# Attention values of a two-layer encoder: the values' projection turned round, with transposes to token order

## The chip, the cores and the metric

The kernel runs on one core of a Trainium2 chip. What is measured is the time of one execution on the device, in microseconds (us); lower is better. The core has a matrix engine (PE), whose loading of stationary operands is shown as an engine of its own (PEld), a vector engine (DVE), a scalar engine (ACT), GpSimd (POOL), and DMA queues that are fed by the sync engine (SP) and by ACT. A matmul holds one operand of at most 128 columns in the array (the stationary one, "weights" of the array) and streams the other through it (the moving one); it writes to PSUM, in banks of 512 float32 per partition. In the profile a matmul is written `out<-moving,stationary`.

## The reference, cut to what matters

Two requests of 512 tokens and 1,024 features go through a two-layer encoder. Layer 0 projects the normed input h with one matrix `w_in` (queries, keys, values, and a Hyena part), lets three groups of four heads attend in dilated windows, and merges the groups:

```python
proj = h @ p['w_in']
qkv = proj[..., :3 * ATTN_WIDTH].reshape(B, L, 3, N_PATTERNS, ATTN_HEADS_PER_GROUP, HEAD_DIM)
for g, (window, dilation) in enumerate(ATTN_PATTERNS):        # (128, 1), (512, 4), (2048, 16)
    o, lse = _dilated_window_attention(qkv[:, :, 0, g], qkv[:, :, 1, g], qkv[:, :, 2, g],
                                       slopes[g], window, dilation)
```

The values of one group are a 1,024 x 256 projection: `ATTN_WIDTH` is 768, `HEAD_DIM` is 64. Layer 1 is an RWKV-7 scan in both directions; each layer ends in a convolutional feed-forward part (FFN). Everything is float32.

## The kernel before

All activations lie feature-major: a tile is 128 features x 512 tokens, and eight tiles make one request's 1,024 features. A projection is `dense` (lines 119 to 130): it loads a block of weights, 128 output features wide, and for each of the eight feature chunks k runs three matmuls, because each float32 operand is split into a high and a low part (`mm3`: high x high, low x high, high x low). Weights are stationary, 512 tokens stream: 24 matmuls per 128 outputs, in one PSUM bank of the pool `psd` (tag `pd`, three banks, shared by both requests). `load_w` (line 97) brings a block of 512 KB by a DMA on ACT's queue into one of two `wraw` buffers; ACT rounds it to the high part `whi`, POOL subtracts to get the low part `wlo`.

Attention (`attention`, line 440) goes through six parts: group g = 0, 1, 2 by head pair hp = 0, 1. `project(g, hp)` makes queries and keys of a part (two calls of `dense`) and, where hp is 0, the values V of the whole group. V is wanted token-major (128 tokens x 256 features, four blocks b), since it is the stationary operand of the product with the attention weights. So the values' projection (lines 453 to 469) swaps the roles: h is stationary, 128 tokens of it at a time, and 256 columns of the weights (`wva`) stream. For g = 0 the 128 tokens of a block lie side by side; for g = 1 and 2 a block takes every fourth token (`perm`, line 343), so the stationary operand is read with a step of four. The four blocks fill two PSUM banks `pv` of the pool `psd`, which are held from the first matmul to the last of the 96, and are then copied to V by ACT (line 469).

`attend` (line 485) makes scores of a head in PSUM (`ps<-qk,qk`), DVE adds the distance penalty into a tile `sb` (three buffers) and takes the row maximum, ACT takes the exponential in place, PE transposes `sb` block by block, the transposed block `pt` is copied out, and PE multiplies it with V (`ps<-pt,V`).

Two requests, s = 0 and 1, run as generators that yield the estimated PE time of what they issued. `weave` and `run` interleave them by these estimates: while part n attends, part n + 1 is projected; beside the attention of request 0 runs the conditioning (`ada_params`, matmuls `ps<-adaw,sc`, fed by 512 KB transfers on SP's queue), and beside that of request 1 the output projection and FFN of request 0. The list of tiles so issued is then ordered once more, engine by engine, by a scheduler that knows each operation's inputs and buffers; within an engine, work is done strictly in that order.

Of the kernel before, what the change touches and what calls it, by code (L numbers as in the profile page):

```python
# [8 lines left out]
F32 = mybir.dt.float32  # L9
# [8 lines left out]
L = 512  # L18
NS = 2
T = NS * L  # L20
KC = D // 128
# [16 lines left out]
def _vec_layout():  # L38
    at = 0
    for name, n in (("adab0", 48), ("adab1", 48), ("n1_0", 8), ("n2_0", 8), ("n1_1", 8), ("n2_1", 8), ("fin", 8),  # L40
# [3 lines left out]
        VEC[name] = at  # L44
        at += n
    return at
# [5 lines left out]
class K:  # L52
# [387 lines left out]
    def attention(self, s, hs, ap, op, then, early):  # L440

        nc, a = self.nc, self.a
        xs = lambda k: hs[k]
        nd = op.tile([128, 3, 4, 2, 4], F32, name="nd")
        z = op.tile([128, 516], F32, name="places")
        nc.sync.dma_start(z, a["places"])
        nm, den = nd[:, :, :, 0], nd[:, :, :, 1]
        rel = ap.tile([128, 640], F32, name="rel")
        nc.sync.dma_start(rel, a["rel"])
        O, V, qk = {}, {}, {}  # L450

        def project(g, hp):
            if hp == 0:
                V[g] = ap.tile([128, 4, 256], F32, tag="V", bufs=2, name="V")
                pv = [self.psd.tile([128, 512], F32, tag="pd", name="pv") for _ in range(2)]
                for i in range(2):
                    wh, wl = self.load_w(a["wva"][g, :, i * 4:i * 4 + 4], 4, 256)
                    for k0 in (0, 2):
                        for b in range(4):
                            o = pv[b // 2][:, b % 2 * 256:b % 2 * 256 + 256]  # L460
                            for k in (k0, k0 + 1):
                                first, last = i + k + b % 2 == 0, i + k == 4
                                hh, hl = (self.perm(t, g, b) for t in hs[i * 4 + k])
                                self.mm(o, hh, wh[k], start=first, stop=False, skip_group_check=True)
                                self.mm(o, hl, wh[k], start=False, stop=False, skip_group_check=True)
                                self.mm(o, hh, wl[k], start=False, stop=last, skip_group_check=True)
                    yield 48 * 109
                for b in range(0, 4, 2):
                    nc.scalar.copy(V[g][:, b:b + 2], pv[b // 2].rearrange("p (b c) -> p b c", b=2))
            qk[g, hp] = []  # L470
            for i, m in enumerate((g * 2 + hp, 6 + g * 2 + hp)):
                t = ap.tile([128, L], F32, tag=f"qk{i}", bufs=2, name=f"qk{i}")
                qk[g, hp].append(t)
                yield from self.dense(a["win"][m], KC, xs, lambda ps: nc.scalar.activation(t, ps, AF.Copy, scale=0.125 if i == 0 else 1.0))

        parts = [(g, hp) for g in range(3) for hp in range(2)]
        yield from project(*parts[0])
        for (g, hp), nxt in zip(parts, parts[1:]):
            yield from self.weave(project(*nxt), self.attend(ap, g, hp, qk[g, hp], V[g], rel, nm, den, O, op))
        early()  # L480
        g, hp = parts[-1]
        yield from self.weave(then, self.attend(ap, g, hp, qk[g, hp], V[g], rel, nm, den, O, op))
        self.at_out = nd, z, O
# [847 lines left out]
def _blocks(np, w, m):  # L1331

    k, n = w.shape
    return np.ascontiguousarray(w.reshape(k // 128, 128, n // m, m).transpose(2, 1, 0, 3))


def layout(np, i):
    _vec_layout()
    o = {}
    x = np.concatenate([i["x_prompt"][0], i["x_sample"][0]], 0)  # L1340
    o["xT"] = np.ascontiguousarray(x.T.reshape(KC, 128, T).transpose(1, 0, 2))
    c = np.concatenate([i["c_prompt"], i["c_sample"]], 0)
    o["cT"] = np.ascontiguousarray(c.T.reshape(KC, 128, NS).transpose(1, 0, 2))
    vec = np.zeros((128, NV), np.float32)

    def put(name, arr, rows=128):
        arr = np.asarray(arr).reshape(-1, rows)
        vec[:rows, VEC[name]:VEC[name] + arr.shape[0]] = arr.T

    for l in range(2):  # L1350
        p = f"l{l}_"
        o[f"adaw{l}"] = _blocks(np, i[p + "ada_w"], 512)
        o[f"up{l}"] = _blocks(np, i[p + "ffn_up"], 128)
        o[f"dn{l}"] = _blocks(np, i[p + "ffn_down"], 128)
        put(f"adab{l}", i[p + "ada_b"])
        put(f"n1_{l}", i[p + "norm1"])
        put(f"n2_{l}", i[p + "norm2"])
        put(f"cw{l}", i[p + "ffn_conv_w"])
        put(f"cb{l}", i[p + "ffn_conv_b"])
    put("fin", i["final_norm"])  # L1360
    put("sw", i["l0_short_w"])
    put("sb", i["l0_short_b"])
    put("fbias", i["l0_filt_bias"])
    for n, m in (("fb1", "filt_b1"), ("fb2", "filt_b2"), ("fb3", "filt_b3"), ("freq", "filt_freq")):
        put(n, i["l0_" + m], 64)
    for n, m in (("mu", "mu"), ("w0", "w0"), ("a0", "a0"), ("kk", "k_k"), ("ka", "k_a"), ("rk", "r_k"), ("lnw", "ln_w"), ("lnb", "ln_b")):
        put(n, i["l1_" + m])
    fw = np.full((8, 128), 2.0 ** -9, np.float32)
    fw[0, 0] = 2.0 ** -10
    fw[4, 0] = 2.0 ** -10  # L1370
    put("fw", fw)
    put("rest", np.where(np.arange(128) % 32 // 4 == 1, -1.0, 0.0).astype(np.float32))
    o["vecs"] = vec
    o["ident"] = np.eye(128, dtype=np.float32)
    w = i["l0_w_in"]
    o["win"] = _blocks(np, w, 128)
    o["wva"] = _blocks(np, w[:, 1536:2304], 256)
    o["wout"] = _blocks(np, i["l0_w_out"], 128)
    for n in "rkvo":
        o["w" + n] = _blocks(np, i["l1_w_" + n], 128)  # L1380
    for n in "wa":
        o[f"l{n}1"] = _blocks(np, i[f"l1_{n}1"].transpose(1, 0, 2).reshape(D, 128), 128)
    g1, g2 = i["l1_g1"], i["l1_g2"]
    o["lg1a"] = _blocks(np, g1[:, :128], 128)
    o["lg1b"] = _blocks(np, g1[:, 128:], 32)

    l2 = np.zeros((6, 128, KC, 128), np.float32)
    for j, m in enumerate((i["l1_a2"], i["l1_w2"])):
        for d in range(2):
            l2[j * 2 + d] = np.concatenate([m[d]] * 2).reshape(128, KC, 128)  # L1390
    l2[4] = g2[:128].reshape(128, KC, 128)
    l2[5, :96] = np.concatenate([g2[128:]] * 3).reshape(96, KC, 128)
    o["l2"] = np.ascontiguousarray(l2.transpose(2, 1, 0, 3))
    for n in ("filt_w1", "filt_w2", "filt_w3", "filt_w4"):
        o[n] = i["l0_" + n]
    o.update(constants(np))
    return o
# [87 lines left out]
```

## Time and profile before

| | us |
|---|---|
| median of three timed runs | 3595.82 |
| lowest and highest of them | 3590.41, 3604.41 |
| profiled execution, its own time | 3581.8 |
| its span, first to last instruction | 3580.0 |
| PE busy | 3311.5 (92%) |
| DVE, ACT, POOL busy | 1707.0, 1576.7, 1603.4 |
| mean granted clock of PE | 0.956 of full speed |

Busy time of PE is the time in which at least one matmul is under way; consecutive matmuls overlap in their ends, so how long one costs is read from the distance of two starts, not from its own duration. Attention of request 0 fills the span from 50 to about 300 us, that of request 1 from 448 to about 850 us, each with other work between.

### The profile page before, as it was taken

The page shows a single profiled execution, that of the slowest core. Times are in us where ns is not written, and L with a number is a line of the kernel's source. Part 1 is how long each engine was busy: PE and PEld are TensorE (multiplying, and loading weights), DVE is VectorE, ACT ScalarE, POOL GpSimd, SP SyncE. Part 2 cuts the span into 40 slices and gives each one's busy share as a digit, 9 for nine tenths or more (in the row PEclk, how much of TensorE's full clock was granted, in tenths as well). Part 3 has the DMA queues.
Part 4 walks back from the last instruction along what each step waited for, and adds up shares of the span by engine and source line. Part 5 has one row for each costly group of instructions (what it writes and reads, how often), then busy time and mean ns, then how long its engine had stood idle before and what let it go on. Part 6 is the DMA issues. An engine that isn't in the chain of part 4 may idle for free. (4 is left out here: it accounts for less than half of the span.)

```text
span 3580.0 us, 62660 instructions
## 1 busy us (share of the span) xinstructions
PE 3311.5 (92%) x24082; PEld 2367.3 (66%) x24082; DVE 1707.0 (48%) x3181; ACT 1576.7 (44%) x3139; POOL 1603.4 (45%) x1480
## 2 busy tenths in 40 slices
PE   7999989999999899999998897798999999989998
PEld 4555767887877676676665564466666666667776
DVE  5021442212335555386677658467677663442223
ACT  3122244434334445545556557444555454443332
POOL 2111342334435665464444557455445443444443
PEclk9999999999999999999998997798999999999999
DMA  7655141222344224654445441574444443342322
GB/s 247 227 188 192 59 136 54 76 71 86 127 132 143 97 95 165 218 155 113 115 126 135 130 121 49 198 250 152 114 113 118 127 106 94 123 159 91 97 89 88
DMA packets 378787, 463.26 MB, mean 129 GB/s; under 512 B 201239, under 2 KB 218903, under 8 KB 377080
## 3 DMA queue, kind: packets, MB, share of 16 engines
q1 hardware_dynamic: 302928, 247.78, 22.7%
q10 hardware_dynamic: 75560, 211.48, 18.6%
q8 instruction: 189, 3.10, 0.4%
q14 instruction: 110, 0.90, 0.1%
HBM read 378.11 MB, written 81.00 MB: 128 GB/s over the span
## 5 line engine op out<-in xcount | busy, mean ns | idle before, releaser
L112 POOL TENSOR_TENSOR wlo<-wraw,whi 128x512 fp32r<-128x512 f32 (+1 forms) x830 | 1086.2, 1313 | 1356.4 <-ACT whi L108 1184.7
L108 ACT CAST whi<-wraw 128x512 fp32r<-128x512 f32 (+1 forms) x830 | 497.5, 606 | 877.3 <-PE pd L78 675.8
L78 PE MATMUL pd<-midh,whi 128*128 128x512 f32 x704 | 287.9, 410 | 6.2 <-ACT midh L141 6.2
L78 PE MATMUL pd<-midl,whi 128*128 128x512 f32 x704 | 282.9, 402 | 0.9 <-DVE midl L144 0.3
L78 PE MATMUL pd<-midh,wlo 128*128 128x512 f32 x704 | 282.4, 402 | 0.3 <-POOL wlo L112 0.3
L328 DVE SCALAR_TENSOR_TENSOR x<-pd,ada,x 128x512 f32<-128x512 f32 x192 | 142.7, 746 | 196.0 <-PE pd L78 195.2
L78 PE MATMUL pd<-xml,whi 128*128 128x512 f32 (+1 forms) x448 | 191.1, 427 | 21.2 <-DVE xml L144 13.7
L78 PE MATMUL pd<-xmh,whi 128*128 128x512 f32 (+1 forms) x448 | 195.4, 438 | 5.5 <-ACT xmh L141 5.4
L78 PE MATMUL pd<-xmh,wlo 128*128 128x512 f32 (+1 forms) x448 | 186.8, 418 | 3.9 <-POOL wlo L112 3.7
L1226 POOL TENSOR_TENSOR Sg<-S,G 128x256 f32<-128x256 f32 x144 | 102.9, 714 | 169.5 <-DVE S L1224 156.2
L291 DVE SCALAR_TENSOR_TENSOR fa<-pd,vecs,fa 128x511 f32<-128x511 f32 x88 | 65.7, 746 | 231.9 <-ACT fa L290 231.9
L1211 ACT COPY UV<-X 32x128 f32<-32x128 f32 x512 | 131.6, 257 | 93.4 <-PE X L78 65.7
L321 DVE TENSOR_TENSOR fa<-fa,pd 128x512 f32<-128x512 f32 x88 | 60.4, 686 | 214.0 <-PE pd L78 202.3
L78 PEld LDWEIGHTS pd<-midh,whi 128*128 128x128 f32 x704 | 132.7, 189 | 40.6 <-ACT midh L141 9.2
L78 PEld LDWEIGHTS pd<-midl,whi 128*128 128x128 f32 x704 | 133.3, 189 | 33.4 <-DVE midl L144 4.2
L78 PEld LDWEIGHTS pd<-midh,wlo 128*128 128x128 f32 x704 | 132.9, 189 | 31.1 <-POOL wlo L112 0.7
L1224 DVE TENSOR_TENSOR S<-X,Sg 128x256 f32<-128x256 f32 x144 | 60.6, 421 | 185.1 <-ACT ys L1222 181.8
L78 PE MATMUL X<-UV,Am 32*32 32x64 f32 (+1 forms) x4096 | 127.5, 228 | 20.3 <-ACT UV L1211 17.4
L1141 DVE TENSOR_TENSOR W<-W,sub 128x120 f32<-128x120 f32 (+7 forms) x496 | 136.3, 275 | 11.1
L78 PEld LDWEIGHTS X<-UV,Am 32*32 32x32 f32 (+1 forms) x4096 | 79.0, 108 | 86.2 <-ACT UV L1211 64.3
L1139 DVE TENSOR_TENSOR sub<-U,W 128x120 f32<-128x120 f32 (+7 forms) x496 | 128.8, 260 | 14.7 <-DMA U<-inv 3.9
L78 PEld LDWEIGHTS pd<-xml,whi 128*128 128x128 f32 (+1 forms) x448 | 88.5, 198 | 53.4 <-DVE xml L144 26.2
(477 smaller groups left out, 8007.0 us busy)
## 6 DMA issues: line engine op xcount, KB each, us to landing
wraw<-in_up ACTq DMA_DIRECT2D x176, 512.0 KB, 3.5
adaw<-in_adaw SPq DMA_DIRECT2D x96, 512.0 KB, 5.2
wraw<-in_dn ACTq DMA_DIRECT2D x128, 256.0 KB, 2.7
wraw<-in_win ACTq DMA_DIRECT2D x36, 512.0 KB, 3.5
x<-x SPq DMA_DIRECT2D x48, 256.0 KB, 3.4
wraw<-in_dn ACTq DMA_DIRECT2D x64, 192.0 KB, 2.4
x<-res SPq DMA_DIRECT2D x32, 256.0 KB, 3.0
wraw<-in_wk ACTq DMA_DIRECT2D x16, 512.0 KB, 3.6
```

What stands on the lines that cost most here:

```text
L78: return self.nc.tensor.matmul(*a, **k)
L108: nc.scalar.copy(h, raw[:, o:o + w])
L112: nc.gpsimd.tensor_tensor(l, raw[:, o + p:o + p + w2], h[:, p:p + w2].bitcast(F32), ALU.subtract)
L291: nc.vector.scalar_tensor_tensor(t[:, 1:], ps[:, :L - 1], w(0), t[:, 1:], ALU.mult, ALU.add)
L321: nc.vector.tensor_tensor(act, act, ps, ALU.mult)
L328: nc.vector.scalar_tensor_tensor(x[m], ps, self.ada[l][:, 40 + m, s:s + 1], x[m], ALU.mult, ALU.add)
L1139: nc.vector.tensor_tensor(w, U4[:, :, k:, e * K + k:e * K + k + 1].to_broadcast(shape), W4[:, e:e + 1, k:k + 1, 0:k + 1].to_broadcast(shap ...
L1141: nc.vector.tensor_tensor(W4[:, :, k:, 0:k + 1], W4[:, :, k:, 0:k + 1], w, ALU.add)
L1211: nc.scalar.copy(dst, X[ur, :, uu(g)])
L1224: nc.vector.tensor_tensor(S, X[:, :, 384:512].rearrange("p d (g v) -> p d g v", g=2), self.Sg, ALU.add)
L1226: nc.gpsimd.tensor_tensor(Sg, S, self.G[:, tau, :, :, None].to_broadcast([128, 2, 2, 64]), ALU.mult)
```

## The change

The values are projected as everything else: weights stationary (blocks 12 to 17 of `win`, 128 columns each, in place of the 256-column blocks `wva`), 512 tokens streaming, 24 matmuls into one `pd` bank. ACT copies the bank to a tile `vt` in the buffers of `sb`; for g = 1 and 2 this copy brings the tokens into the order of the blocks, reading PSUM with a step of four. Four transposes on PE turn `vt` to token order in a `ps` bank, and DVE copies that into half of V. This is done twice per group.

```diff
-                pv = [self.psd.tile([128, 512], F32, tag="pd", name="pv") for _ in range(2)]
                 for i in range(2):
-                    wh, wl = self.load_w(a["wva"][g, :, i * 4:i * 4 + 4], 4, 256)
-                    for k0 in (0, 2):
-                        for b in range(4):
-                            o = pv[b // 2][:, b % 2 * 256:b % 2 * 256 + 256]
-                            for k in (k0, k0 + 1):
-                                first, last = i + k + b % 2 == 0, i + k == 4
-                                hh, hl = (self.perm(t, g, b) for t in hs[i * 4 + k])
-                                self.mm(o, hh, wh[k], start=first, stop=False, skip_group_check=True)
-                                self.mm(o, hl, wh[k], start=False, stop=False, skip_group_check=True)
-                                self.mm(o, hh, wl[k], start=False, stop=last, skip_group_check=True)
-                    yield 48 * 109
-                for b in range(0, 4, 2):
-                    nc.scalar.copy(V[g][:, b:b + 2], pv[b // 2].rearrange("p (b c) -> p b c", b=2))
+                    vt = ap.tile([128, L], F32, tag="sb", bufs=3, name="vt")
+                    yield from self.dense(a["win"][12 + g * 2 + i], KC, xs, lambda ps: nc.scalar.copy(self.unperm_src(vt, g), self.unperm(ps, g)))
+                    ps = self.ps()
+                    for b in range(4):
+                        self.tr(ps[:, b * 128:b * 128 + 128], vt[:, b * 128:b * 128 + 128], self.ident)
+                    nc.vector.tensor_copy(V[g][:, :, i * 128:i * 128 + 128], ps.rearrange("p (b c) -> p b c", b=4))
+                    yield 440
```

On PE, where the values of g = 1 of request 0 begin, the order before is this (`adam` belongs to the conditioning):

```order
L81 MATMUL ps<-ident,adam 128x128 x4
L78 MATMUL pd<-h7h,wlo 128x512
L78 MATMUL pv<-whi,h0h 128x256
L78 MATMUL pv<-whi,h0l 128x256
L78 MATMUL pv<-wlo,h0h 128x256
L78 MATMUL pv<-whi,h1h 128x256
L78 MATMUL pv<-whi,h1l 128x256
L78 MATMUL pv<-wlo,h1h 128x256
```

At the same place of the changed kernel stands:

```order
L78 MATMUL pd<-h0h,whi 128x512
L78 MATMUL pd<-h0l,whi 128x512
L81 MATMUL ps<-ident,adam 128x128 x4
L78 MATMUL pd<-h0h,wlo 128x512
L78 MATMUL pd<-h1h,whi 128x512
L78 MATMUL pd<-h1l,whi 128x512
L78 MATMUL pd<-h1h,wlo 128x512
```

The operands have changed sides, the matmuls are half as many and twice as wide; where one group of values took 96 of them, it takes 48.

A little further on PE, where group 0 of request 0 attends (`qk_...` are its keys and queries), stood before, between scores and transposes, matmuls of the values:

```order
L81 MATMUL ps<-ident,sb 128x128 x3
L78 MATMUL ps<-qk_696,qk_645 128x256
L78 MATMUL pv<-whi,h4h 128x256
L78 MATMUL pv<-whi,h4l 128x256
L78 MATMUL ps<-pt,V 64x128 x3
L78 MATMUL ps<-adaw,sc 32x512 x2
L81 MATMUL ps<-ident,sb 128x128 x2
L78 MATMUL ps<-qk_696,qk_645 128x256
```

For the second head of that part the changed kernel has:

```order
L78 MATMUL ps<-qk_669,qk_611 128x256
L78 MATMUL pd<-h7h,wlo 128x512
L81 MATMUL ps<-ident,sb 128x128 x2
L78 MATMUL ps<-qk_669,qk_611 128x384
L78 MATMUL ps<-pt,V 64x128 x2
L81 MATMUL ps<-ident,sb 128x128 x3
L78 MATMUL ps<-adaw,sc 32x512
L78 MATMUL ps<-pt,V 64x128 x3
L78 MATMUL ps<-adaw,sc 32x512 x3
L78 MATMUL ps<-qk_669,qk_611 128x384
L78 MATMUL ps<-adaw,sc 32x512 x4
L81 MATMUL ps<-ident,sb 128x128 x3
```

Here two pairs of scores and their transposes have moved together: one matmul stands between them, or two short ones.

The transposes of `vt` stand further on still, among those of `sb`:

```order
L78 MATMUL ps<-adaw,sc 32x512
L81 MATMUL ps<-ident,sb 128x128 x2
L81 MATMUL ps<-ident,vt 128x128 x4
L78 MATMUL ps<-qk_863,qk_734 128x256
L78 MATMUL ps<-pt,V 64x128 x2
L78 MATMUL ps<-adaw,sc 32x512 x3
```

They come long after the 24 matmuls of their block. From the FFN of request 0 at 1,087 us of the profile before (a `pd<-h0h,whi` on PE) to the end, every engine's instructions stand in the same order in both kernels.

## Rows read from the trace of the kernel before

**Rows 1.** The page: busy us of each engine, share of the span, instructions.

```profile
PE 3311.5 (92%) x24082; PEld 2367.3 (66%) x24082; DVE 1707.0 (48%) x3181; ACT 1576.7 (44%) x3139; POOL 1603.4 (45%) x1480
```

**Rows 2.** Busy time of each engine in stretches from 83 to 1087 us.

```profile
core 0: us, PE busy (x) PEld busy (x) DVE busy (x) ACT busy (x) POOL busy (x), PEclk, DMA share, GB/s
83.00:125.00 42.00, 42.00 (x168) 19.85 (x167) 0.28 (x2) 8.53 (x16) 10.22 (x8) 1.00 0.82 294
125.00:172.00 47.00, 47.00 (x196) 30.60 (x197) 5.72 (x12) 8.84 (x20) 5.09 (x4) 1.00 0.63 218
...
530.00:590.00 60.00, 57.80 (x258) 46.98 (x257) 13.86 (x26) 21.90 (x41) 14.76 (x12) 1.00 0.15 53
...
680.00:735.00 55.00, 54.43 (x229) 47.18 (x228) 9.22 (x16) 22.21 (x45) 15.27 (x12) 0.97 0.17 58
735.00:1087.00 352.00, 352.00 (x1590) 280.42 (x1589) 106.32 (x163) 124.18 (x222) 150.04 (x123) 0.99 0.33 109
```

**Rows 3.** Matmuls into pv alone, two halves of a projection (g = 0, 2).

```profile
447.90:459.80 11.90, 7.46 (x48) 7.21 (x48) 0.00 (x0) 0.86 0.73 229
682.50:693.80 11.30, 11.28 (x48) 11.22 (x48) 0.00 (x0) 1.00 0.28 94
```

**Rows 4.** Weight loads of pv: ns minimum/median/maximum.

```profile
L78 PEld LDWEIGHTS pv<-whi,h0h x24: 186/329/334, 49.6 to 686.5; 128*128 128x128 f32 x24
```

**Rows 5.** Starts on PE, values of g = 0, request 1.

```profile
457.14 0.28 PE L78 MATMUL pv<-wlo,h2h 128*128 128x256 f32 x1
...
459.63 0.28 PE L78 MATMUL pv<-wlo,h3h 128*128 128x256 f32 x1
459.75 0.39 PE L78 MATMUL pd<-mx0h,whi 128*128 128x512 f32 x1
```

**Rows 6.** Matmuls into pd alone, one dense block (queries).

```profile
693.75:699.34 5.59, 5.58 (x24) 4.33 (x24) 0.00 (x0) 0.00 (x0) 1.00 0.00 0
```

**Rows 7.** Four transposes between dense matmuls, starts on PE.

```profile
124.07 0.60 PE L81 MATMUL ps<-ident,adam 128*128 128x128 f32 x4
124.43 0.49 PE L78 MATMUL pd<-h7h,wlo 128*128 128x512 f32 x1
124.75 0.28 PE L78 MATMUL pv<-whi,h0h 128*128 128x256 f32 x1
```

**Rows 8.** The transposes of sb, grouped by line.

```profile
L81 PE MATMUL ps<-ident,sb 128*128 128x128 f32 x144 | 30.3, 283 | 4.1 <-ACT sb L527 4.1
```

**Rows 9.** PE's waits inside the values' projection of request 1, g = 0.

```profile
454.00 0.58 PE L78 MATMUL pv<-whi,h0h 128*128 128x256 f32 x1 [4.35 <-DVE res L283]
...
463.73 0.47 PE L78 MATMUL pd<-mx0h,whi 128*128 128x512 f32 x1 [0.93 <-DVE res L283]
```

**Rows 10.** One score tile from matmul to exponential, in order of time.

```profile
154.77 0.70 PE L78 MATMUL ps<-qk,qk 64*128 64x256 f32 x2
...
155.40 0.51 PE L78 MATMUL pv<-whi,h4h 128*128 128x256 f32 x1
...
156.90 0.19 ACT L527 ACTIVATION_READ_ACCUMULATOR sb<-sb,nd 128x1 f32 x1
```

**Rows 11.** PE's waits from 480 to 735 us: total, times, longest.

```profile
PE ps L81 <- ACT sb L527: 4.1, 3, 2.2
```

**Rows 12.** Score tiles on DVE, and evacuations on ACT.

```profile
L503 DVE SCALAR_TENSOR_TENSOR sb<-rel,ps x32: 409/482/555, 133.8 to 614.1; 128x256 f32<-128x256 f32 x16, 128x384 f32<-128x384 f32 x16
L514 DVE SCALAR_TENSOR_TENSOR sb<-rel,ps 128x512 f32<-128x512 f32 x16 | 11.0, 688 | 84.5 <-PE ps L78 84.5
L469 ACT COPY V<-pv x12: 580/586/591, 82.7 to 734.1; 128x512 f32<-128x512 f32 x12
L521 ACT COPY O<-ps x12: 586/1072/1097, 195.1 to 848.8; 128x512 f32<-128x512 f32 x12
```

**Rows 13.** Transfers of the values' weights and of the blocks beside them.

```profile
L103 ACTq DMA_DIRECT2D wraw<-in_win x36: 329/334/405, 19.4 to 889.6; - x36
...
L103 ACTq DMA_DIRECT2D wraw<-in_wva x12: 333/335/445, 7.6 to 698.6; - x12
```

More of the change, by code (lines that the diff above doesn't have):

```diff
@@ L1376, in layout @@
     o["win"] = _blocks(np, w, 128)
-    o["wva"] = _blocks(np, w[:, 1536:2304], 256)
     o["wout"] = _blocks(np, i["l0_w_out"], 128)
```

## The prediction

> **What bounds the kernel now.** I read the page's list of engines first, then the stretches in which attention runs, then the starts of single matmuls. PE is busy for 92% of the span and no other engine for half of it [rows 1]. By stretches it is plainer: with request 0 attending and the conditioning beside it, PE is busy for all of 47 us; with request 1 attending beside the FFN of request 0, for 57.80 of 60 and 54.43 of 55 us; DVE, ACT and POOL are at half or under there; and after the last attention PE is busy for all of the 352 us up to 1,087 [rows 2]. So a microsecond that PE no longer works in attention is a microsecond of the span, unless something new makes PE wait. Behind 1,087 us every engine's instructions stand in the same order in both kernels, as the section on the change says; so whatever is gained or lost by then is carried to the end unchanged, and only the part ahead has to be worked out.
>
> The busy time doesn't say what a matmul costs, the starts do. Of the projection of values, 48 matmuls of g = 2 take 11.28 us, 0.235 us each, while the 48 of g = 0 are started within 7.46 us of busy time [rows 3], and where nothing holds them up 0.119 us apart: 22 steps from 457.14 to 459.75 [rows 5]. They are the same shapes and stream the same 256 columns. What differs is the stationary operand, read with a step of four tokens: its load takes 186 ns at least and 329 ns in the median [rows 4], since two groups of three are strided. The stride doubles the matmul. A dense matmul of 512 columns, with contiguous weights, costs 5.58 us for 24, 0.233 us each [rows 6]: no more than a strided one of half the width. That is the whole case for the change.
>
> **The change part by part.**
>
> *Matmuls removed.* Each group of each request has 96 matmuls of values; two groups of two requests are strided. 4 x 96 x 0.235 = 90.2 us [rows 3]. Two are contiguous: 2 x 96 x 0.119 = 22.8 us [rows 5].
>
> *Matmuls added.* Six times two dense blocks at 5.58 us [rows 6]: 44.6 us in place of the strided 90.2, and 22.3 us in place of the contiguous 22.8. Together -45.6 - 0.5 = -46.1 us. The columns streamed are as many as before (96 x 256 and 48 x 512), so nothing can be saved beyond the stride.
>
> [...]
>
> *Transposes added.* Eight per group, 48 in all, in twelve lots of four. Four transposes between dense matmuls take 0.36 us from the first to the next matmul, and that next matmul takes 0.32 us in place of 0.23 [rows 7]: 0.45 us a lot, 5.4 us in all. Were they not pipelined at all, each would cost its own 283 ns [rows 8], 13.6 us; were the change of shape free, 4.3 us. I take 5.4, from the lot that stands among the same neighbours. By the order they stand long after their block's last matmul, so they don't wait for the copy to `vt`.
>
> [...]
>
> *Copies.* ACT copied V twelve times at 0.586 us; it now makes twelve copies to `vt`, eight with a stride, for which the nearest row is the strided copy of O at 1.07 us [rows 12]. At most 4 us more, on an engine busy for 8.84 of 47 us and 22.21 of 55 [rows 2]. DVE gets twelve copies that it had not; a 512-wide pass of DVE over PSUM takes 0.688 us [rows 12], so 8.3 us over two stages where it is busy for 5.72 of 47 and 9.22 of 55. Both lie beside PE's matmuls and cost nothing by themselves. In ACT's queue the copy to `vt` delays exponentials by a microsecond, which counts among the waits below.
>
> *Weights.* Twelve transfers of 512 KB as before, from `win` in place of `wva`, issued by the same queue [rows 13]; rounding on ACT and POOL stays. Nothing.
>
> *PSUM.* `pv` held two of the three `psd` banks through 96 matmuls. Where request 1 begins, its second bank had to wait 4.35 us for a bank of the output projection, and that projection 0.93 us in its turn [rows 9]. Now a block takes one bank. I take off 3 us of the 5.3, because the block now wants all eight chunks of h at once, which are still being made there; bounds -5.3 and 0.
>
> *Waits added.* The new tile `vt` sits in a buffer of `sb`, of which there are three, from its copy to its transposes, and the scores of `attend` need these. Also, the filler between scores and transposes is shorter. From the end of a score's matmul (PE starts its next work at 155.40) to the end of its exponential (156.90 + 0.19) are 1.7 us [rows 10]. In the changed order two of the scores of request 0, second head of g = 0, have only one dense matmul (0.23 us) or two short ones (some 0.3) ahead of their transposes; PE waits there for some 1.4 us each, and all that is queued behind on PE waits too. Everywhere else I count work for about two microseconds or more. That makes +3 us. Bounds: 0, if ACT is early; and +10, if ten such places each lose a microsecond to ACT's new copies (the longest such wait before is 2.2 us, three of them 4.1 us together [rows 11]).
>
> *Sum.* -46.1 + 5.4 - 3 + 3 = -40.7 us. The profiled execution took 3581.8 us (span 3580.0 and 1.8 around it), so 3541 for a like execution. The timed runs have a median of 3595.8, 14 us above the profiled one; the difference is taken over to that: 3595.8 - 40.7 = 3555 us, 1.1% faster. By the outer bounds of the terms (-46.1 + 4.3 - 5.3 + 0 and -46.1 + 13.6 + 0 + 10) it is 3549 to 3573.
>
> **The rivals.**
>
> *More is freed.* In the stretches of strided values, matmuls between other work cost more than the steps counted (busy time before and after each change of shape, a dense matmul 0.32 in place of 0.23 [rows 7]), and there are half as many now; if of 192 changes of neighbour some 100 vanish at 0.09 us, that is 9 us more, and with the full 5.3 of the banks the time is 3595.8 - 40.7 - 9 - 2.3 - 3 (no new waits) = 3541. For it: values and other work are finely mixed in request 0. Against: the other work has to stand somewhere, and finds dense matmuls as neighbours there.
>
> *The conditioning's transfers become the bound.* Request 0's stage would shrink by some 20 us while it still fetches the same megabytes. Its 47 us with g = 1 moved 218 GB/s at 0.63 of the DMA's time; shortened by 10 us that is 277 GB/s. If transfers can't go faster, request 0 gains nothing and request 1 alone gains 20: 3576. Against: the stretch just ahead moved 294 GB/s with PE busy for all of its 42 us [rows 2].
>
> *The score chain takes it back (slower).* There are 48 score tiles [rows 12]. If `vt` in the buffers of `sb` makes each tile wait for the one before, PE loses up to the chain of 1.7 us where its filler ends. The gain of 40.7 us is eaten from 0.85 us per tile on; at 1.2 us per tile the time is 3595.8 - 40.7 + 58 = 3613. For it: three buffers become one while two `vt` are held, and two places already show it. Against: the other 46 tiles have dense matmuls, the conditioning or the FFN of the other request between score and transpose.
>
> *The stride is not what costs.* If the 256 columns and not the stride made the 0.235 us, matmuls would be saved nowhere and the transposes and waits added: 3595.8 + 5.4 + 3 - 3 = 3601. The contiguous group with its 0.119 us speaks against it [rows 5]. [...]
>
> **How the numbers follow.** Forecast 70%, more freed 12%, transfers 12%, score chain 4%, stride not the cause 2%. A change of this kernel's time can be told from none beyond about 0.5%, 18 us; its three runs lie 14 us apart. Faster by more than that (below 3578): the forecast, the case of more, and most of the transfers' case, 0.92. Within: the rest of that case, and a part of the last two, 0.05. Slower: 0.03. The range has to hold the forecast's bounds, the better case and the transfers' case nearly: 3540 to 3577.
>
> **What would show it.** In the profile after: no `pv`; twelve times 24 matmuls into `pd` with blocks of `win`, 0.23 us apart, and no weight load of 329 ns beside them; the attention of request 0 over about 20 us earlier, and the FFN's `pd<-h0h,whi` now at 1,087 us at about 1,046, and from there every row earlier by the same amount. Lots of transposes into `ps` from `vt`, 0.36 us each, with no wait ahead. Two waits of PE of over a microsecond for ACT's `sb` in the conditioning's stretch. I am wrong if the dense matmuls of values are started further apart than those of queries, if PE waits for `adaw`, if waits for `sb` sum to over 10 us, or if the shift at 1,046 us is not the shift at the end.

## The result, and the profile after

The changed kernel takes 3543.84 us (median of four runs, 3529.60 to 3563.24), the kernel before in the same series 3593.36 (four runs, 3590.41 to 3604.41). The ratio is 0.9856, with a 95% interval of 0.9826 to 0.9887: 1.4% faster. The forecast was 3555 in a range of 3540 to 3577, from a gain of 40.7 us; the gain measured is 49.5, and the time lies 4 us above the lower end of the range. Timed twice more the changed kernel took 3547.45 us (ratio 0.9881, interval 0.9842 to 0.9919) and 3543.80 us (0.9866, 0.9846 to 0.9886).

The page's list of engines, changed kernel, which answers to [rows 1]: PE has 240 matmuls fewer and is busy for 42.8 us less; the others are as they were.

```profile
PE 3268.7 (92%) x23842; PEld 2309.3 (65%) x23842; DVE 1711.8 (48%) x3193; ACT 1578.4 (45%) x3141; POOL 1601.7 (45%) x1480
```

The matmuls into `pd` alone, in the stretch of one dense block of values (g = 2, request 1), by window:

```profile
core 0: us, PE busy (x) PEld busy (x) DVE busy (x) ACT busy (x), PEclk, DMA share, GB/s
655.19:660.78 5.59, 5.59 (x26) 4.51 (x24) 0.69 (x1) 0.00 (x0) 1.00 0.29 94
```

5.59 us for 24 matmuls, as the queries had [rows 6]; the 48 strided matmuls that did half of the same work before took 11.28 [rows 3]. A lot of transposes of `vt` on PE, starts in order of time:

```profile
459.34 0.39 PE L78 MATMUL pd<-mx3h,wlo 128*128 128x512 f32 x1
459.58 0.60 PE L81 MATMUL ps<-ident,vt 128*128 128x128 f32 x4
459.93 0.47 PE L78 MATMUL pd<-h0h,whi 128*128 128x512 f32 x1
460.24 0.39 PE L78 MATMUL pd<-h0l,whi 128*128 128x512 f32 x1
```

0.35 us to the next matmul and 0.31 for that one, nothing ahead: as in [rows 7]. The two copies that go with it, grouped by line (ns minimum/median/maximum):

```profile
L457 ACT COPY vt<-pd x12: 577/585/592, 77.9 to 693.5; 128x512 f32<-128x512 f32 x12
...
L461 DVE COPY V<-ps x12: 676/690/692, 91.0 to 699.6; 128x512 f32<-128x512 f32 x12
```

Eight of ACT's twelve read PSUM with a step of four, and all cost the 0.585 us of a copy in order. PE's waits from 40 to 350 us (total, times, longest), and the place of the two longest on PE's timeline:

```profile
PE ps L81 <- ACT sb L520: 3.8, 3, 1.5
PE ps L78 <- DMA adaw<-in_adaw: 2.3, 3, 1.1
PE ps L78 <- ACT hw L403: 1.6, 1, 1.6
```

```profile
168.63 0.70 PE L78 MATMUL ps<-qk,qk 64*128 64x256 f32 x2
169.25 0.50 PE L78 MATMUL pd<-h7h,wlo 128*128 128x512 f32 x1
171.00 0.44 PE L81 MATMUL ps<-ident,sb 128*128 128x128 f32 x2 [1.25 <-ACT sb L520]
171.36 0.91 PE L78 MATMUL ps<-qk,qk 64*128 64x384 f32 x2
172.20 0.65 PE L78 MATMUL ps<-pt,V 128*64 128x128 f32 x4
174.32 0.90 PE L81 MATMUL ps<-ident,sb 128*128 128x128 f32 x3 [1.46 <-ACT sb L520]
```

A pair of scores, one dense matmul, and then transposes that have to wait for the exponential: this is the place that the order showed ahead of the run. Where request 1 begins ([rows 9] before), PE's waits from 413 to 483 us are now:

```profile
PE pd L78 <- DVE r L257: 3.1, 1, 3.1
PE pd L78 <- POOL wlo L112: 1.4, 2, 0.7
PE pd L78 <- ACT whi L108: 1.3, 1, 1.3
```

No bank is waited for; a norm's `r`, weights and, with 2.2 us in five smaller groups, chunks of activations are.

Where the time went is read from places that stand alike in both kernels. The end of request 0's attention (`ps<-nd,places`; its last products with V start at 376.69 us in the profile before, so it lasts longer than the 300 us named in the section on time) and the FFN of request 0 on PE, before:

```profile
397.37 2.86 PE L78 MATMUL ps<-nd,places 128*128 128x16 f32 x25
...
1086.06 0.79 PE L78 MATMUL pd<-h0h,whi 128*128 128x512 f32 x1
```

and after:

```profile
380.46 3.64 PE L78 MATMUL ps<-nd,places 128*128 128x16 f32 x32
...
1038.45 0.39 PE L78 MATMUL pd<-h0h,whi 128*128 128x512 f32 x1
```

16.9 us are gained by the end of request 0's attention, and 47.6 by the FFN. (Over the two profiles of before and the three of the changed kernel that the experiments give, `ps<-nd,places` starts 20.4 us sooner in the mean: 397.37 and 398.68 against 380.46, 376.51 and 375.79.) Yet the span is only 40.6 us shorter (3539.4 against 3580.0), though behind that place all engines do the same work in the same order. The experiments turned to this too.

### The profile page after: what moved, and what is told of

Its sections match the earlier page's. It is cut to its first block, busy times and chain, and to the rows that moved or that the text cites. A ratio compares the mean times of both kernels' runs of the same rounds, so it can differ in the third digit from the quotient of the medians.

```text
span 3539.4 us, 62176 instructions
## 1 busy us (share of the span) xinstructions
PE 3268.7 (92%) x23842; PEld 2309.3 (65%) x23842; DVE 1711.8 (48%) x3193; ACT 1578.4 (45%) x3141; POOL 1601.7 (45%) x1480
## 5 line engine op out<-in xcount | busy, mean ns | idle before, releaser
L78 PEld LDWEIGHTS pd<-midl,whi 128*128 128x128 f32 x704 | 133.9, 190 | 34.3 <-DVE midl L144 5.2
```

The source lines that it names most:

```text
L78: return self.nc.tensor.matmul(*a, **k)
```

## Experiments

"The marker" below is one subtraction on POOL in the stretch after the last attention, `wlo<-wraw,whi`, the 1,146th-last operation of POOL in every kernel. Before it stands at 1174.08 us, in the changed kernel at 1126.96. "Tail" is the span from there to the end.

| run | marker | tail | median us (runs) | ratio, 95% interval |
|---|---|---|---|---|
| before, profile ahead of the prediction | 1174.1 | 2405.9 | | |
| before again, e3_before | 1180.1 | 2412.7 | 3593.60 (8) | 1.0001 [0.9980, 1.0023] |
| changed kernel | 1127.0 | 2412.5 | 3543.84 (4) | 0.9856 [0.9826, 0.9887] |
| again, e2_after | 1128.2 | 2414.1 | 3547.45 (4) | 0.9881 [0.9842, 0.9919] |
| again, e11_after | 1127.1 | 2423.4 | 3543.80 (4) | 0.9866 [0.9846, 0.9886] |
| e1_contig | 1121.6 | 2417.6 | 3551.73 (4) | 0.9898 [0.9854, 0.9941] |
| e10_step2 | 1129.3 | 2419.5 | 3548.63 (4) | 0.9872 [0.9852, 0.9893] |
| e12_step3 | 1158.0 | 2416.4 | 3566.88 (4) | 0.9901 [0.9862, 0.9940] |
| e7_moving_strided | 1174.9 | 2416.4 | 3591.23 (10) | 0.9990 [0.9971, 1.0009] |
| e5_pv_ps | 1180.1 | 2426.5 | 3597.59 (10) | 1.0016 [0.9999, 1.0032] |
| e4_vt_own | 1131.6 | 2418.3 | 3536.75 (4) | 0.9849 [0.9811, 0.9888] |
| e8_vt_own_again | 1124.2 | 2408.4 | 3536.93 (4) | 0.9842 [0.9819, 0.9866] |
| e6_strided_only | 1123.5 | 2415.7 | 3538.33 (4) | 0.9837 [0.9812, 0.9862] |
| e9_both | 1136.6 | 2406.8 | 3545.56 (6) | 0.9873 [0.9853, 0.9893] |

### The stride alone taken away (e1_contig)

The kernel before, in which the values of g = 1 and 2 take tokens that lie side by side (V is then that of other tokens); the order of all instructions is that of before.

```diff
-                                hh, hl = (self.perm(t, g, b) for t in hs[i * 4 + k])
+                                hh, hl = (self.perm(t, 0, b) for t in hs[i * 4 + k])
```

> The kernel before, in which the values of g = 1 and 2 take their 128 stationary tokens side by side instead of every fourth (V then holds other tokens than the reference wants); order, shapes, banks, copies and waits for buffers are those of before. Theory (the stride of the stationary operand is the cost): the 384 matmuls go from 0.235 to 0.119 us, 44.5 us less; the first FFN row that stood at about 1,087 us stands at about 1,042, median about 3549 us. Rival (256-column matmuls cost this much, or the gain came from the freed PSUM bank): PE's starts stay 0.235 us apart, and the time stays within 5 us of the kernel before.

The weight loads of the values, and the window that answers to the second of [rows 3]:

```profile
L78 PEld LDWEIGHTS pv<-whi,h0h x24: 186/188/330, 47.3 to 646.3; 128*128 128x128 f32 x24
```

```profile
644.28:650.04 5.76, 5.76 (x48) 5.71 (x47) 0.00 (x0) 1.00 0.29 94
```

The median load falls from 329 to 188 ns and 48 matmuls from 11.28 to 5.76 us, with not one instruction changed otherwise. That is the stride, shown. The marker comes 52 us sooner than in the first profile of before, more than the 44.5 that the steps give. PE stood at the lower of its two granted clock levels (0.5 of full speed) for 17.2 us ahead of the marker in this profile and for 34.3 us in that one of before; how much two executions of one kernel differ, the next runs show.

### The same kernels again (e2_after, e3_before, e11_after)

Nothing is edited.

> The changed kernel once more. It was 47 us ahead of the kernel before at the start of the FFN that follows attention, and 40.6 us ahead at the end, with the same order in between. Theory (the clock's half-speed windows fall elsewhere in each execution): the FFN's start comes at 1,040 us again within 2 us, while what lies behind it takes another length than 2,499 us, by 3 us or more, longer with more time at half clock. Rival (the later stages systematically give 6 to 7 us back): 2,499 us again within 1 us.

> The kernel before once more, for a second profile of it. What is open: the changed kernel reached the FFN of request 0 47 us sooner than before did but ended only 40.6 us sooner, though behind that place the order of work is the same. If the tail's length depends on the execution and its clock alone, this profile will have another tail than 2,405.9 us (from the first subtraction of wlo from wraw in that FFN on POOL to the end of the span), between 2,406 and 2,418 as the changed kernels had, and the row that stood at 1,174.1 us stands there again within 2 us. If the change itself makes what follows slower, the tail is again 2,406 within 2 us, against 2,412.4 and 2,414.0 of the two profiles of the changed kernel.

> The changed kernel a third time, on the chip and beside the runs of the variants. If the variants' 5 to 10 us are theirs, it stays at 3543 to 3548 us with the variant at 3535 to 3540, and waits for sb of 3.8 us stand in the conditioning's stretch. If they were spread, its median comes down to within 4 us of the variant's. The tail behind the FFN's first subtraction of wlo should lie between 2,406 and 2,418 us again, as in all kernels whose later part is the same.

The marker on POOL's timeline in the second profile of before:

```profile
1180.10 1.71 POOL L112 TENSOR_TENSOR wlo<-wraw,whi 128x512 fp32r<-128x512 f32 x1
```

and the stretch behind the marker in the first and the third profile of the changed kernel, by windows:

```profile
1127.00:3539.00 2412.00, 2192.53 (x19131) 1559.97 (x19131) 1347.12 (x2604) 1157.06 (x2334) 1207.90 (x1146) 0.94 0.43 128
```

```profile
1127.00:3550.00 2423.00, 2207.70 (x19132) 1569.32 (x19131) 1346.30 (x2604) 1156.47 (x2334) 1207.02 (x1147) 0.93 0.43 127
```

The same 19,131 matmuls of one kernel keep PE busy for 15 us more in one execution than in the other, at a mean clock of 0.93 against 0.94, and the tail is 11 us longer. The second profile of before has a tail of 2412.7, as the changed kernel's first two; its marker is 6 us later than in the first, where I had expected it within 2. So the 6 to 7 us that seemed to be given back behind the FFN belong to the first profile of before, which had the shortest tail of all. With e2_after alone this stayed open, since its tail is 1.6 us from the first; e3_before decides it, for the execution, and e11_after went 5 us beyond the bounds that I had given the tail. All the profiles say the same: the tails of the six profiles with the old projection in every group have a mean of 2416.4 us, those of the six with the new one in every group 2415.5. The two longest, 2426.5 and 2423.4 (e5_pv_ps, e11_after), have PE at the lower clock level for 344 and 334 us; two of the three shortest, 2405.9 and 2408.4 (before, e8_vt_own_again), for 283 and 282. The third, e9_both, has 308 us in 2406.8, so the clock is not all of it.

The marker of the changed kernel stands at 1127.0, 1128.2 and 1127.1, of before at 1174.1 and 1180.1: the difference of the means is 49.7 us, and the median times differ by 49.5. The gain by the FFN is the gain at the end. The spans of these five profiles differ by 42.4 us in the mean, and those of the pair by 40.6: with so few profiles the spread of the tails, 20 us, hides the rest.

### Where the price of a stride begins (e10_step2, e12_step3)

As e1_contig, but with every second token, and with every third one of the first 384:

```diff
-                                hh, hl = (self.perm(t, g, b) for t in hs[i * 4 + k])
+                                hh, hl = (t.rearrange("p (h i r) -> p h r i", h=2, r=2)[:, b // 2, b % 2] if g else self.perm(t, g, b) for t in hs[i * 4 + k])
```

```diff
-                                hh, hl = (self.perm(t, g, b) for t in hs[i * 4 + k])
+                                hh, hl = (t[:, :384].rearrange("p (i r) -> p r i", r=3)[:, b % 3] if g else self.perm(t, g, b) for t in hs[i * 4 + k])
```

> The kernel before with the values of groups 1 and 2 reading every second token in place of every fourth (the output is then that of other tokens); order of all instructions as before. What is told apart is on what the price of the stride depends. If it goes with the distance between the elements that are read, a strided matmul costs about half way between 0.119 and 0.235 us, 0.17 to 0.18, the FFN row comes some 23 us sooner, at 1,150 to 1,157, and the time is 3570. If any step costs the same, the steps are 0.235 us, the row stays at 1,174 to 1,180 and the time at 3593. If a step of two is free as one is, the row comes at 1,122 and the time is 3551, as with tokens side by side.

> The kernel before with the values of groups 1 and 2 reading every third token of the first 384 (the output is then that of other tokens); order of all instructions as before. A step of two cost nothing (3548.6 us, matmuls 0.12 us apart, the FFN row at 1,129), a step of four doubles the matmul (0.235). If the price begins where the distance of two elements reaches that of four (16 bytes), a step of three is free as well: 0.12 us, the row at 1,122 to 1,130, the time 3548. If it begins behind two and grows, or doubles at once, the matmuls are 0.18 to 0.235 us apart, the row stands at 1,150 to 1,180 and the time between 3570 and 3593.

48 matmuls of values (g = 2, request 1) by window, with a step of two:

```profile
649.68:655.49 5.81, 5.81 (x48) 5.76 (x47) 0.00 (x0) 1.00 0.30 93
```

with a step of three, and the loads there:

```profile
670.30:678.62 8.32, 8.32 (x48) 8.28 (x48) 0.00 (x0) 1.00 0.30 92
```

```profile
L78 PEld LDWEIGHTS pv<-whi,h0h x24: 186/256/268, 48.8 to 673.3; 128*128 128x128 f32 x24
```

A step of two is free (0.121 us a matmul, against 0.120 in e1_contig), three costs 0.173, four 0.235 [rows 3]. My first guess for three, that the price begins at 16 bytes between two elements, fell; from two on it goes nearly with the step, as 2 to 3 to 4. (Spacing and time of three, 0.173 and 3566.88 us, lie just under the bounds of 0.18 and 3570 that I had given the other case.) The markers order themselves likewise: 1121.6, 1129.3, 1158.0, 1174.1.

### The stride on the moving side (e7_moving_strided)

The changed kernel, with the step of four put into the 512 moving columns of the values' blocks, and the copy to `vt` in order:

```diff
-                    yield from self.dense(a["win"][12 + g * 2 + i], KC, xs, lambda ps: nc.scalar.copy(self.unperm_src(vt, g), self.unperm(ps, g)))
+                    yield from self.dense(a["win"][12 + g * 2 + i], KC, lambda k: [self.unperm(t, g) for t in hs[k]], lambda ps: nc.scalar.copy(vt, ps))
```

> The changed kernel, with the order of tokens for g = 1 and 2 made by the matmul: the 512 moving columns of h are read with a step of four tokens, and ACT copies the bank as it lies. Order and everything else as in the changed kernel. Theory A (only loads of the stationary operand suffer from the step): the matmuls stay 0.23 us apart, the FFN's start is within 1 us of e2. Theory B (PE suffers from any read of SBUF with that step): 192 matmuls twice as long, 45 us later at the FFN's start, median about 3590 us.

The block that took 5.59 us, by window and by starts on PE:

```profile
685.30:696.12 10.82, 10.82 (x26) 4.95 (x24) 0.69 (x1) 0.00 (x0) 1.00 0.28 97
```

```profile
687.82 0.64 PE L78 MATMUL pd<-h1h,wlo 128*128 128x512 f32 x1
688.28 0.64 PE L78 MATMUL pd<-h2h,whi 128*128 128x512 f32 x1
```

0.46 us a matmul in place of 0.23, with weights that lie side by side and are loaded in 0.21 us there. All of the gain is gone (ratio 0.999). So it isn't the load alone that pays, as I had thought; turning the projection round helped only because the step was moved off PE's reads, to ACT's copy, which takes the 0.585 us of a copy in order.

### The banks of PSUM (e5_pv_ps)

The kernel before, with `pv` from the pool `ps`:

```diff
-                pv = [self.psd.tile([128, 512], F32, tag="pd", name="pv") for _ in range(2)]
+                pv = [self.ps("pv") for _ in range(2)]
```

> The kernel before with the two banks pv of the values taken from the pool ps in place of psd; matmuls, strides and copies as before. What is told apart is the term of the PSUM banks, -3 us with bounds -5.3 and 0. If the bank is what PE waited for where request 1 begins, the waits of 4.35 and 0.93 us for DVE's res are gone or short there and the row of the FFN that was at 1,174.1 us comes 3 to 5 us sooner, the time 3589 us. The rival: the chunks of h that are made at that moment bind instead, other waits take their place, or the pool ps with two banks fewer makes scores and the conditioning wait: then the FFN comes at 1,172 or later, and the time is the same as before or some us longer.

PE's waits from 430 to 500 us, where [rows 9] had 4.35 and 0.93 for a bank:

```profile
PE pd L78 <- ACT whi L108: 2.8, 1, 2.8
PE pv L78 <- POOL wlo L112: 2.3, 2, 1.4
PE pd L78 <- ACT mx3h L141: 0.8, 1, 0.8
```

and from 40 to 350 us:

```profile
PE ps L78 <- DMA adaw<-in_adaw: 9.6, 5, 3.5
PE ps L78 <- ACT hw L403: 5.7, 1, 5.7
PE ps L81 <- ACT sb L527: 4.9, 5, 2.0
```

The waits for `res` are gone and others, for weights, stand in their place: all of PE's waits in that stretch sum to 6.2 us, against 8.9 before. Half of the bank's 5.3 us is lost at once to what is late next, and the two banks fewer in `ps` cost more than the rest beside the conditioning, where PE's waits sum to 21.6 us, against 3.4 and 4.9 in the two profiles of before. The rival of that expectation held. The changed kernel itself has 8.0 us of waits in the same stretch; from the start of `ps<-nd,places` to the first score of request 1 it takes 103.8 to 106.6 us in its three profiles, and 103.7 and 105.3 in the two of before. e6_strided_only (below) keeps group 0's banks in `psd` and PE's waits of 4.3 and 0.9 us for `res`, and takes 100.9: freeing the banks brought nothing there.

### Buffers of its own for vt (e4_vt_own, e8_vt_own_again)

```diff
-                    vt = ap.tile([128, L], F32, tag="sb", bufs=3, name="vt")
+                    vt = ap.tile([128, L], F32, tag="vt", bufs=2, name="vt")
```

> The changed kernel with two buffers for vt alone, so that it takes none from the score tiles sb; the scheduler then puts 8 to 10 dense matmuls between the score matmuls and transposes that stood together. Theory (the tile vt costs waits through the buffers of sb): PE's waits for sb between 40 and 350 us, 3.8 us in the changed kernel, fall under 1 us and the FFN's start comes 3 to 4 us sooner than in e2. Rival (PE is held there by the conditioning's transfers anyway): the waits go to adaw, and the FFN's start is within 1 us of e2.

> The changed kernel with vt in buffers of its own once more: its median was 3536.8 us against 3543.8 and 3547.5 for the changed kernel, while its profile reached the FFN no sooner (1,131.6 us against 1,127.0 and 1,128.2). If the buffers are worth something, the time is 7 us or more under the changed kernel's again, 3534 to 3540, and the FFN row comes at 1,126 or sooner. If that was the spread from execution to execution, the time is 3540 to 3550, and the FFN row between 1,126 and 1,132; the waits for sb in the conditioning's stretch are gone in either case.

No wait for `sb` is left in the conditioning's stretch in either profile, where the changed kernel had 3.8, 3.8 and 3.3 us in its three. The marker stands at 1131.6 and 1124.2, on both sides of the changed kernel's; the first fits neither case of e4_vt_own's expectation. Both medians are 7 to 11 us under the changed kernel's, and the second run met the expectation of a gain on both counts; but the intervals overlap, and e9_both below has the same buffers and shows none: beside its 3545.56 us the changed kernel took 3543.80 in the same series (e11_after), within the 4 us that were to mean spread. That the waits go is shown; whether time is gained by it stays open.

### The change in the strided groups alone (e6_strided_only), and with those buffers (e9_both)

```diff
-                pv = [self.psd.tile([128, 512], F32, tag="pd", name="pv") for _ in range(2)]
+                if g == 0:
+                    pv = [self.psd.tile([128, 512], F32, tag="pd", name="pv") for _ in range(2)]
...
+                else:
+                    for i in range(2):
+                        vt = ap.tile([128, L], F32, tag="sb", bufs=3, name="vt")
...
```

In e9_both `vt` has the tag and the two buffers of e4_vt_own besides.

> The change in groups 1 and 2 alone; the values of group 0, whose tokens lie side by side, are projected in the old way. By the theory that the stride is the whole gain, group 0 brought 0.5 us less the four of twelve lots of transposes (1.8 us) and the banks (3 us and what lay beside them): the FFN row at 1,130 us, 1 to 4 us behind the changed kernel's 1,127.0 and 1,128.2, the time 3545 to 3551. The rival, that more is freed by wide matmuls in general (the gain was 47 us there, and 41 was worked out): the contiguous group had a share in it, and this kernel reaches the FFN 6 us or more behind the changed one, at 1,133 or later, the time 3552 or more.

> The change in groups 1 and 2 alone, and vt in two buffers of its own: the two variants that came out lowest (3538.3 and 3536.8 and 3536.9 us) in one kernel. If the buffers take away waits that group 0's old route doesn't already avoid, the waits for sb in the conditioning's stretch (1.5 us) go, and the FFN row comes at 1,120 to 1,122, the time 3533 to 3537. If both had avoided the same waits, it is within the spread of the two: the FFN row at 1,122 to 1,126, the time 3535 to 3542.

Without group 0 the change is worth as much: 3538.33 us, the marker 4 us ahead of the changed kernel's, where I had expected it 1 to 4 behind. The wide matmuls as such bring nothing that group 0 would show: values, dense blocks and transposes of `vt`, summed from start to start from 45 us to the marker, take 784.1 us here and 782.1 to 784.2 in the changed kernel's three profiles. The 4 us are found in the conditioning (below). That the two variants add up fell: e9_both came out above both of its expectations, at the changed kernel's time. In its profile PE waits 5.1 us for `adaw` beside the conditioning, the changed kernel 1.8 to 2.4, and stands at the lower clock level for 57.5 us ahead of the marker, the changed kernel for 31.0 to 44.5; what of this the kernel causes is open.

A part of why kernels that do nearly the same work differ is seen in the conditioning's matmuls. Each lot of them in the order is cut from four that go to different 32 partitions of a bank; the trace shows every matmul as two records (384 of `ps<-adaw,sc` for 192 matmuls). Two lots of before, on PE, one of one matmul and one of four:

```profile
194.97 1.04 PE L78 MATMUL ps<-adaw,sc 128*32 128x512 f32 x2
195.95 0.50 PE L78 MATMUL pd<-h4h,whi 128*128 128x512 f32 x1
```

```profile
190.46 1.06 PE L78 MATMUL ps<-adaw,sc 128*32 128x512 f32 x8
191.46 0.50 PE L78 MATMUL pd<-h2h,wlo 128*128 128x512 f32 x1
```

0.98 us for one and 1.00 for four. What these matmuls cost goes with the number of lots, and that is the scheduler's doing: from 45 us to the end of request 0's attention there are 84 lots before (and in e10_step2, whose order is the same), 75 in each of the three profiles of the changed kernel, 72 in e6_strided_only, 79 in e9_both and 81 in e8_vt_own_again. Summed from start to start these 320 records take 83.0 us in the two profiles of before, 77.4 in those of the changed kernel, 72.6 in e6_strided_only and 80.5 in e8_vt_own_again; e5_pv_ps is out of line with 81.8 for 69 lots, its waits for `adaw` and 30.7 us at the lower clock level among them. In e8_vt_own_again the 3.1 us more eat most of the 3.8 us of waits for `sb` that its buffers took away, so request 0 gained nothing there.

## Why the prediction was right, point by point

*The bound, and the stride.* PE sets the time, and the stride was the price: 329 to 188 ns for the load and 11.28 to 5.76 us for 48 matmuls with nothing else changed. Between the first profile of before and e10_step2, in which PE stood at the lower of its granted clock levels (0.5 of full speed) for 34.3 and 34.0 us ahead of the marker, the marker moves by 44.8 us; 384 matmuls by 0.235 - 0.121 are 43.8. The rival that the stride costs nothing fell. The loads of the same 128 columns took 188, 198, 256 and 329 ns in the median of `pv<-whi,h0h` with steps of 1, 2, 3 and 4 (e1_contig, e10_step2, e12_step3, [rows 4]), by the step alone.

*Dense matmuls, transposes, copies.* 5.59 us against 5.58 a block; 0.35 and 0.31 us at a lot of transposes against 0.36 and 0.32; copies of 0.585 and 0.690 us, with the bound of 1.07 for a strided one not reached. The row of O that gave this bound was not of the same kind: its copy reads PSUM in order and writes SBUF with the step of four (line 521 of the kernel before), that of `vt` reads PSUM with the step and writes in order.

*Waits.* 3 us were worked out, two of 1.4 at the second head of group 0; 3.8 came, two of 1.25 and 1.46 there and one of 1.05 (182.08 us) besides. What the term left out is request 1: the three waits for `sb` there, 4.1 us [rows 11], shrank to one. From 400 to 1,090 us the changed kernel has

```profile
PE ps L81 <- ACT sb L520: 0.5, 1, 0.5
```

Over both requests waits for `sb` thus grew by some 0.2 us, not by 3. The slower rival, a score chain by the buffers of `sb`, would have needed 0.85 us at each of 48 tiles to eat the gain.

*Transfers.* Waits for `adaw` are 2.3 us, against 1.7 before: request 0 gained its part (16.9 us in the pair of profiles, 20.4 in the mean of five; half of the matmuls' terms and six lots of transposes are 17.3 when the three microseconds of waits are added). This rival fell. I had written that I'd be wrong if PE waited for `adaw`; it did before as well, and half a microsecond more is no sign of anything.

*The banks.* This step failed: "I take off 3 us of the 5.3". The time between the attentions is what it was. The row named a bank as what came last; the rounded weights, the chunks of h and a norm were hardly earlier, and PE waits for these now: 8.0 us in place of 8.9.

*The size.* 40.7 us were worked out and 49.5 measured. Summed from start to start, from 45 us to the marker and as a mean over the profiles of each kernel, the values' matmuls took 133.0 us before, and dense blocks take 85.6 us more now: -47.4, waits and banks between them included, for a term of -46.1 with -3 and +3. Transposes +5.1 for +5.4. With PE's idle time taken out, the two are -46.8 us together, so the term of the matmuls was right. PE's idle time between 45 us and the marker sums to 28.7 us in both profiles of before and to 29.3, 26.0 and 27.7 in those of the changed kernel: -3 and +3 came to nothing, as forecast, but neither was right by itself. What was left out stands elsewhere: -5.6 us by nine lots fewer in the conditioning. Scores (-1.7), products with V (+1.9) and transposes of `sb` (-1.1) nearly cancel, and the first of these is the waits for `sb` that went. The change gave the scheduler other pieces to place, and the other pieces fell better; nothing in the forecast counted them, so for it this part of the gain is luck. In the forecast every matmul that the diff doesn't touch had its old price; one of the rivals spoke of neighbours, and by 3541 us came out nearest. Of its three reasons the banks did not hold, the neighbours of the values' matmuls did not either (-46.8 for -46.1, where it had 9 us more), and no new waits held in the sum alone.

*The shift to the end.* That the shift at 1,046 us is the shift at the end was a good test badly measured: with one profile of each it failed by 7 us (47.6 and 40.6); the markers of five profiles and the medians of the timed runs agree within a microsecond (49.7 and 49.5).

## What to carry to other kernels

Look at the spacing of matmuls of one shape with operands that are read with different steps: if the strided ones stand further apart, move the step to an engine with idle time, an evacuation above all, on the side that reads PSUM (0.585 us here with the step as without), and don't merely swap the operands: the strided moving operand paid too (0.46 us in place of 0.23). Before counting on a wait to vanish, look up what is late next at the same place, and when a change makes a scheduler deal its pieces anew, count the pieces of the neighbours' work as well. A difference of 7 us between two profiles of 3,560 us is what two executions of one kernel differed by here (tails of 2405.9 and 2412.7 us for before); take the shift at a place in common from several profiles.

## What the hardware showed beyond that

- With a stationary operand of 128 columns in float32, 256-column matmuls start as close together with a step of two as with one (0.121 us in e10_step2, 0.120 in e1_contig), and from there the matmul takes time with the step: 0.121, 0.173 and 0.235 us for steps of 2, 3 and 4. Why a step of two costs nothing and a step of three does, no run shows.
- A moving operand with a step of four doubled the matmul as well, 0.23 to 0.46 us for 512 columns (e7_moving_strided).
- ACT reads PSUM with a step of four at 0.585 us for 512 columns, as in order. With the step on the side that writes SBUF the copy took 1.07 us: of the twelve copies of O [rows 12] the four of group 0, in order, take 0.586 to 0.589, the eight strided ones 1.070 to 1.097.
- One to four matmuls of the conditioning into different 32 partitions of a bank took 0.98 to 1.00 us together. So a matmul that stands alone cost about what a lot of four did: in the kernel before 84 lots stood where 320 records of 160 matmuls would make 40. By these rows 35 lots fewer than the changed kernel's 75 would be worth up to 34 us of PE, an estimate; whether the transfers of `adaw` could keep up is open, and it wasn't tried.
